# Three edits to the order of loads, weight splits and products between a hybrid layer's out-projection and its first feed-forward matrix

## The chip, the cores and the metric

The kernel runs on 1 core of one Trainium2 chip. Its time is the device time of one execution in microseconds (us). One matmul instruction is issued after the other on TensorE (PE); VectorE (DVE), ScalarE (ACT) and GpSimd (POOL) prepare its operands and take its results; SyncE (SP) issues most loads, and ACT and POOL issue some of the stores.

## The reference

One decoder layer on x of 2048 tokens by 1024 channels, float32:

```python
def rmsnorm(x, g):
    r = lax.rsqrt(jnp.mean(xf * xf, axis=-1, keepdims=True) + EPS)
    return xf * r * g
...
h = rmsnorm(x, g1)
mixed = concat(mLSTM heads (chunkwise, stabilised) * gate, S5 state space * GLU)
x = x + mixed @ w_out                                # out-projection
x = x + square(relu(rmsnorm(x, g2) @ w1)) @ w2       # feed-forward, 4096 wide
return rmsnorm(x, gf)
```

All products are kept at about float32 accuracy: each operand is split into a high part (a rounded copy, made by ACT) and a low part (operand minus high part, made by DVE or POOL), and each product is the sum of three matmuls, high by high, high by low, low by high.

## The kernel before

The program has four stages: the mixer, then the out-projection with the second norm, then the first feed-forward matrix (FFN1), then the second one (FFN2) with the final norm. A tile scheduler sets the order in which each engine runs its instructions, from the order of the code and from its own estimates; so code that is moved changes the order on engines other than those it names. Buffers come from pools of fixed size, and a load into a buffer waits for the last reader of what was in it.

**Out-projection.** Four tiles of 512 tokens (`o_tile(t)`), in each four column blocks `j` of 256, so 16 units of 96 matmuls (L913 to L915) that accumulate into `po` and are added to x (L917). The weights of a unit come from `wunit` (L91): for t = 0 a raw 1 MB load (`wraw`, one buffer in this stage), two copies by ACT into `whi` (L103), and two subtractions into `wlo` (L108), the first half of the columns on POOL and the second on DVE; then `whi` and `wlo` are written to DRAM (W_dx, L111 and L112). For t = 1 to 3, `whi` and `wlo` are loaded from there (L96, L97), 2 MB for a unit. `whi` and `wlo` have two buffers each. The results of a tile go to DRAM by four writes that POOL issues (X_d, L919). Behind tiles 0 and 1 stands `first_norm`, which normalises, transposes and splits the operands of the first half of FFN1 (B11, B21, T1, T2, B22), and writes two more, T3 and T4, to DRAM (HT_d, L961).

**FFN1.** Two halves of the tokens, 16 f-blocks in each (`ff1(half, f)`, L1017), and in each f-block seven products of blocks in place of eight (a Strassen-Winograd scheme), every one 12 matmuls of 512 columns into one PSUM bank (`pf`, L1046 to L1048): 84 matmuls. The products go by the operand of the token side: B11, B21, T1, T2, B22, T3, T4. The weight side of an f-block is one 1 MB load (`raw`, L1020, one buffer); four sums of its quarters on DVE (`sw`, L1033 to L1037); and splits (L866 on ACT, L867 on DVE): `wa` for the products with B11 and B21, `wb` for T1 and T2, `wc` for B22 and T3, and `wd`, from a quarter of `raw` itself, for T4, each with one buffer. The seventh product of an f-block (T4) with the work behind it (`rest`) is put on a list, and `fourth()` runs it in the next f-block, behind the products with B11 and B21; at the end of each half `fourth()` is called once more. Results leave for DRAM by stores that ACT issues, three of 256 KB for `c` and one of 1 MB for `ss` (A_d, L1087). Ahead of the first f-block the code loads T3 and T4 (`sg`, L1095, eight loads of 256 KB) and the norm's weights `gb` (L1097). Between the halves the operands of the second half (`hraw`, L1107, seven loads of 1 MB through two buffers) are loaded and split with one instruction of 2048 columns for each part.

Of the kernel before, what the change touches and what calls it, by code (L numbers as in the profile page):

```python
# [43 lines left out]
def tile_hybrid_block(ctx, tc, x, xT, wqk, wv, wo, wu, wglu, wout, w1, w2,  # L44
# [47 lines left out]
    def wunit(src, n, lo_eng, parts=2, key=None, keep=False):  # L92
        hi = wp.tile([P, 2080], F32R, tag="whi", name="whi")
        lo = wp.tile([P, 2080], F32R, tag="wlo", name="wlo")
        if key in split_d:
            Y.dma_start(out=hi[:, :n].bitcast(F32), in_=split_d[key][0])  # L96
            Y.dma_start(out=lo[:, :n].bitcast(F32), in_=split_d[key][1])  # L97
            return hi, lo
        raw = wraw(src, n)
        h = n // parts  # L100
        for i in range(parts):
            s = slice(i * h, (i + 1) * h)
            S.activation(hi[:, s], raw[:, s], AF.Copy)  # L103
            e = lo_eng[i % len(lo_eng)]
            q = h // 1 if e is G else h
            for j in range(0, h, q):
                s = slice(i * h + j, i * h + j + q)
                e.tensor_tensor(lo[:, s], raw[:, s], hi[:, s].bitcast(F32), op=SUB)  # L108
        if keep:
            split_d[key] = dram.tile([2, P, n], F32, name=f"W_d{key}")  # L110
            Y.dma_start(out=split_d[key][0], in_=hi[:, :n].bitcast(F32))  # L111
            Y.dma_start(out=split_d[key][1], in_=lo[:, :n].bitcast(F32))  # L112
        return hi, lo
# [777 lines left out]
    def o_tile(loaded):  # L891
        t, mxs, mdma = loaded
        xts = []
        for j in range(4):
            wh, wl = wunit(wout[j].rearrange("p k n -> p (k n)"), 2048, (G, V), key=f"x{j}", keep=t == 0)
            if j == 0:
                for c in range(NC):
                    i = (0, 1, 4, 5, 2, 3)[(4 * t + c) % 6]
                    xt = oa[i // 2].tile([P, DM], F32, tag=f"acc{i}", name="acc")
                    with tc.issue_after(mdma.ins):  # L900
                        Y.dma_start(out=xt, in_=x[t * TT + c * P:t * TT + (c + 1) * P, :])
                    xts.append(xt)
            wh = wh[:, :2048].rearrange("p (k n) -> p k n", k=KD)
            wl = wl[:, :2048].rearrange("p (k n) -> p k n", k=KD)
            js = slice(j * 256, (j + 1) * 256)
            pss = [bank_a("po") for _ in range(NC)]
            for ks in ([(0, 4), (4, 8)] if j in (0, 3) else [(0, 8)]):
                for c in range(NC):
                    cs = slice(c * P, (c + 1) * P)
                    for k in range(*ks):  # L910
                        o = pss[c][:, 0:256]
                        ah, al = mxs[k]
                        T.matmul(o, ah[:, cs], wh[:, k, :], start=(k == 0), stop=False)  # L913
                        T.matmul(o, ah[:, cs], wl[:, k, :], start=False, stop=False)  # L914
                        T.matmul(o, al[:, cs], wh[:, k, :], start=False, stop=(k == 7))  # L915
            for c in range(NC):
                V.tensor_tensor(xts[c][:, js], pss[c][:, 0:256], xts[c][:, js], op=ADD)  # L917
        for c in range(NC):
            G.dma_start(out=X1_d[t][c], in_=xts[c])  # L919
        return xts  # L920
# [61 lines left out]
    with ExitStack() as st:  # L982
# [21 lines left out]
            for i, n in enumerate(OPS):  # L1004
                G.dma_start(out=HD_d[i][:, :, cs], in_=sg[n])

        last = []
        nf = [0]

        def bank_f():  # L1010
            nf[0] += 1
            return ps_.tile([P, TT], F32, tag="gsn"[nf[0] % 3], name="pf")

        def fourth():
            if last:
                last.pop()()

        def ff1(half, f):
            raw = rwp.tile([P, 4, TT], F32, tag="raw", name="raw")
            Y.dma_start(out=raw, in_=w1[f])  # L1020
            sw = rwp.tile([P, 4, TT], F32, tag="sw", name="sw")
            a11, a12, a22, a21 = [raw[:, i] for i in range(4)]
            s1, s2, s4, s3 = [sw[:, i] for i in range(4)]
# [31 lines left out]
            def add(o, ps, c):  # L1055
                V.tensor_tensor(o, ps, c, op=ADD)  # L1056

            def keep(i, c):
                S.dma_start(out=A_d[half][f // 4][i][:, f % 4, :], in_=c)
# [4 lines left out]
            add(c11, prod("12", "B21"), u)  # L1064
            sq(c11)
            keep(0, c11)
            fourth()
            p5 = prod("S1", "T1")
            add(u, prod("S2", "T2"), u)
            add(c12, p5, u)  # L1070
# [8 lines left out]
            V.tensor_tensor(ss[:, 1], ss[:, 0], c11, op=SUB)  # L1079
            V.tensor_tensor(ss[:, 2], c11, c12, op=SUB)  # L1080

            def rest():
                add(c21, prod("22", "T4"), u)
                sq(c21)
                keep(1, c21)
                V.tensor_tensor(ss[:, 3], c21, ss[:, 1], op=SUB)
                S.dma_start(out=A_d[half][f // 4][3:7, :, f % 4, :].rearrange("i p n -> p i n"), in_=ss)  # L1087
            last.append(rest)

        gb = stg.tile([P, DM], F32, tag="gb", name="gb")  # L1090
        for i, n in enumerate(("T3", "T4")):
            H[n] = pair(hb, n)
# [3 lines left out]
                split(*[x[:, :, c * P:(c + 1) * P] for x in H[n]], sg)  # L1096
        Y.dma_start(out=gb, in_=g2v[0].partition_broadcast(P))  # L1097
        for f in range(NF):
            ff1(0, f)
            if f % 2 == 1 and f < 8:  # L1100
                chunk2(f // 2)
        stg_cm.__exit__(None, None, None)
        fourth()
        stg = fpool("st1", 2)
        for i, n in enumerate(OPS):
            raw = stg.tile([P, 4, TT], F32, tag="hraw", name="hraw")
# [2 lines left out]
            split(*H[n], raw)  # L1109
        for f in range(NF):  # L1110
            ff1(1, f)
        fourth()
    right_cm.__exit__(None, None, None)
    ps_cm.__exit__(None, None, None)

# [176 lines left out]
```

## Time and profile before

| | |
|---|---|
| median of 3 runs | 2285.95 us (2281.8 to 2290.44) |
| profiled execution | 2285.07 us, span from first to last instruction 2283.3 us |
| mean granted TensorE clock, share of full speed | 0.976 |
| busy, share of the span | PE 94%, DVE 70%, ACT 41%, POOL 14% |
| chain that ended last, by engine | PE 58%, DMA 17%, DVE 16%, issue 4%, ACT 3% |
| stages, us from the start of the span | mixer to 740, out-projection to 961, FFN1 from 978 to 1637, FFN2 from 1645 |

A stage with a busy PE is bound by the number of matmuls; what an edit to the order can change is the time in which PE has nothing to do or runs at its lower clock. So the waits of PE, what ended them, and the granted clock after them are the rows to look at, stage by stage. A share of DMA near 1.0 in a stretch says that its 16 engines were moving data all the time.

### The profile page before, as it was taken

The numbers are of one execution on the slowest core, as the hardware profiler recorded it, in microseconds if no ns is written. First come the engines' busy times: TensorE is split into PE (matmuls) and PEld (weight loads), VectorE is DVE, ScalarE is ACT, GpSimd is POOL, SyncE is SP. The second block draws the span as 40 slices with busy tenths as digits, with TensorE's granted clock in tenths as the row PEclk, the third lists the DMA queues.
The fourth block names the chain that finished last, engine by engine and source line by source line (L and its number), as shares of the span: only waits on it lengthen the run. The fifth ranks groups of instructions, "written<-read, shape, count | busy, mean of one in ns | idle before, by whom it ended". The sixth has DMA issues, their size and how long they took to land.

```text
span 2283.3 us, 29089 instructions
## 1 busy us (share of the span) xinstructions
PE 2157.2 (94%) x11092; PEld 1821.9 (80%) x11092; DVE 1601.0 (70%) x2286; ACT 943.4 (41%) x1368; POOL 309.5 (14%) x307
## 2 busy tenths in 40 slices
PE   8889999999999999889999999999899999999997
PEld 6677888897887899767777777777688888788886
DVE  8966777775666447167776776666666779877688
ACT  5454434333444322055454554444443334533333
POOL 3674333121121101001100000000000000000000
PEclk9989999999999899989999999999999999999999
DMA  6488677776666877646564553444754344744332
GB/s 237 132 224 258 210 243 253 242 213 209 211 219 226 326 301 298 242 154 227 182 214 147 196 195 117 143 146 152 252 229 160 143 148 166 275 149 153 149 122 92
DMA packets 182467, 454.14 MB, mean 199 GB/s; under 512 B 53140, under 2 KB 82340, under 8 KB 151480
## 3 DMA queue, kind: packets, MB, share of 16 engines
q1 hardware_dynamic: 141784, 367.28, 48.2%
q10 hardware_dynamic: 35360, 67.18, 7.7%
q0 software_dynamic: 5184, 17.83, 2.0%
q8 instruction: 87, 1.43, 0.3%
q14 instruction: 52, 0.43, 0.1%
HBM read 311.56 MB, written 140.66 MB: 198 GB/s over the span
## 4 chain that ended last, share of the span: by engine, by line
PE 58%; DMA 17%; DVE 16%; issue 4%; ACT 3%; POOL 1%; SPq 1%; ACTq 0%; DVEq 0%; POOLq 0%
PE pp L1168 9%; PE pp L1167 9%; PE pp L1166 9%; DMA raw<-in_w 8%; PE pf L1046 4%; PE pf L1048 4%; PE pf L1047 4%; PE po L915 2%; PE po L913 2%; PE po L914 2%; DMA whi<-W_dx 2%; PE pg L792 2%; PE pg L793 1%; DVE w1l L867 1%; PE pg L794 1%
## 5 line engine op out<-in xcount | busy, mean ns | idle before, releaser
L1056 DVE TENSOR_TENSOR c<-pf,c 128x512 f32<-128x512 f32 x224 | 153.4, 686 | 79.4 <-PE pf L1048 74.8
L1172 DVE TENSOR_TENSOR m<-pp,m 128x1024 f32<-128x1024 f32 x96 | 116.8, 1219 | 97.0 <-PE pp L1168 96.9
L1166 PE MATMUL pp<-b0h,a0h 128*128 128x512 f32 x448 | 173.8, 392 | 7.4 <-ACT a0h L866 7.4
L1167 PE MATMUL pp<-b1l,a1h 128*128 128x512 f32 x448 | 177.1, 395 | 2.4 <-DVE b1l L867 2.4
L1168 PE MATMUL pp<-b0h,a0l 128*128 128x512 f32 x448 | 175.1, 392 | 1.8 <-DVE a0l L867 1.8
L1168 PE MATMUL pp<-b1h,a1l 128*128 128x512 f32 x448 | 176.8, 395 | 0.0
L1167 PE MATMUL pp<-b0l,a0h 128*128 128x512 f32 x448 | 175.5, 392 | 0.0
L1166 PE MATMUL pp<-b1h,a1h 128*128 128x512 f32 x448 | 174.8, 395 | 0.0
L118 PE MATMUL pg<-whi,hTh 128*128 128x260 f32 (+1 forms) x512 | 152.3, 297 | 6.9 <-DVE Gt L191 6.1
L1202 POOL TENSOR_TENSOR rr<-rr,cst 128x2 f32<-128x2 f32 x8 | 6.0, 756 | 1107.0 <-DVE rr L1201 1097.1
L913 PE MATMUL po<-whi,mxh 128*128 128x256 f32 x512 | 147.6, 290 | 7.4 <-DMA whi<-W_dx 4.9
L119 PE MATMUL pg<-wlo,hTh 128*128 128x260 f32 (+1 forms) x512 | 150.5, 294 | 0.0
L915 PE MATMUL po<-whi,mxl 128*128 128x256 f32 x512 | 146.7, 289 | 4.0 <-DVE mxl L887 4.0
L120 PE MATMUL pg<-whi,hTl 128*128 128x260 f32 (+1 forms) x512 | 150.0, 293 | 0.0
L914 PE MATMUL po<-wlo,mxh 128*128 128x256 f32 x512 | 146.9, 288 | 0.0
L866 ACT ACTIVATE a1h<-af 128x2048 fp32r<-128x2048 f32 x28 | 53.7, 1919 | 180.8 <-PE pp L1167 152.5
L866 ACT ACTIVATE w1h<-raw 128x1024 fp32r<-128x1024 f32 x64 | 53.9, 844 | 171.2 <-DMA raw<-in_w 128.1
L866 ACT ACTIVATE a0h<-af 128x2048 fp32r<-128x2048 f32 x28 | 53.7, 1918 | 163.1 <-PE pp L1167 148.3
L1052 ACT ACTIVATE c<-c 128x512 f32<-128x512 f32 x128 | 80.2, 628 | 93.6 <-DVE c L1056 91.8
L118 PEld LDWEIGHTS pg<-whi,hTh 128*128 128x128 f32 x512 | 100.3, 196 | 9.3 <-DVE Gt L191 6.8
L913 PEld LDWEIGHTS po<-whi,mxh 128*128 128x128 f32 x512 | 99.9, 195 | 8.9 <-DMA whi<-W_dx 3.4
L1166 PEld LDWEIGHTS pp<-b0h,a0h 128*128 128x128 f32 x448 | 84.8, 189 | 25.5 <-ACT a0h L866 7.8
(370 smaller groups left out, 6146.5 us busy)
## 6 DMA issues: line engine op xcount, KB each, us to landing
af<-A_d SPq DMA_DIRECT2D x56, 1024.0 KB, 4.8
raw<-in_w SPq DMA_DIRECT2D x32, 1024.0 KB, 6.6
A_d<-ss ACTq DMA_DIRECT2D x32, 1024.0 KB, 8.5
A_d<-c ACTq DMA_DIRECT2D x96, 256.0 KB, 3.4
fB<-in_w SPq DMA_DIRECT2D x24, 1024.0 KB, 5.5
xraw<-in_xT SPq DMA_DIRECT2D x27, 512.0 KB, 5.0
whi<-W_dq SPq DMA_DIRECT2D x12, 1024.0 KB, 5.8
wlo<-W_dq SPq DMA_DIRECT2D x12, 1024.0 KB, 5.5
```

Of the source, the lines that this page charges most:

```text
L118: T.matmul(ps, ah, bh, start=(i == 0), stop=False)
L119: T.matmul(ps, ah, bl, start=False, stop=False)
L120: T.matmul(ps, al, bh, start=False, stop=(i == n - 1))
L866: S.activation(hi, src, AF.Copy)
L913: T.matmul(o, ah[:, cs], wh[:, k, :], start=(k == 0), stop=False)
L914: T.matmul(o, ah[:, cs], wl[:, k, :], start=False, stop=False)
L915: T.matmul(o, al[:, cs], wh[:, k, :], start=False, stop=(k == 7))
L1056: V.tensor_tensor(o, ps, c, op=ADD)
L1166: T.matmul(o, ah[:, k, cs], bh[:, k, :], start=(k == 0), stop=False)
L1167: T.matmul(o, ah[:, k, cs], bl[:, k, :], start=False, stop=False)
L1168: T.matmul(o, al[:, k, cs], bh[:, k, :], start=False, stop=(k == 3))
L1172: e.tensor_tensor(o, s, o, op=ADD)
```

## The change

Three parts. In `o_tile`, `wunit` loses its key: the weights of each of the 16 units are loaded raw and split anew, nothing is written to W_dx and nothing is loaded from it. In `ff1`, the seventh product and the work behind it stand at the end of their own f-block, and `fourth()` and its list are gone. And the raw weights of the first f-block are loaded (`raw0`) in the code ahead of the loads of T3, T4 and `gb`.

```diff
@@ o_tile
-            wh, wl = wunit(wout[j].rearrange("p k n -> p (k n)"), 2048, (G, V), key=f"x{j}", keep=t == 0)
+            wh, wl = wunit(wout[j].rearrange("p k n -> p (k n)"), 2048, (G, V))
@@ ff1
-        def fourth():
-            if last:
-                last.pop()()
-
-        def ff1(half, f):
+        def w1_load(f):
             raw = rwp.tile([P, 4, TT], F32, tag="raw", name="raw")
             Y.dma_start(out=raw, in_=w1[f])
+            return raw
+
+        def ff1(half, f, raw=None):
+            raw = w1_load(f) if raw is None else raw
...
             sq(c11)
             keep(0, c11)
-            fourth()
             p5 = prod("S1", "T1")
...
-            def rest():
-                add(c21, prod("22", "T4"), u)
-                sq(c21)
-                keep(1, c21)
-                V.tensor_tensor(ss[:, 3], c21, ss[:, 1], op=SUB)
-                S.dma_start(out=A_d[half][f // 4][3:7, :, f % 4, :].rearrange("i p n -> p i n"), in_=ss)
-            last.append(rest)
-
+            add(c21, prod("22", "T4"), u)
+            sq(c21)
+            keep(1, c21)
+            V.tensor_tensor(ss[:, 3], c21, ss[:, 1], op=SUB)
+            S.dma_start(out=A_d[half][f // 4][3:7, :, f % 4, :].rearrange("i p n -> p i n"), in_=ss)
+
+        raw0 = w1_load(0)
         gb = stg.tile([P, DM], F32, tag="gb", name="gb")
...
-            ff1(0, f)
+            ff1(0, f, raw0 if f == 0 else None)
...
-        fourth()
         stg = fpool("st1", 2)
```

What it makes of the order is seen at three places. The first is the queue of SP at the passage from the out-projection (L86 to L97, and `wraw`, are its weights) to FFN1 (`raw` is the weight load of an f-block, `sg` the loads of T3 and T4 from HT_d, `xt` a load for the norm of the second half). Before:

```order
L97 DMA wlo<-W_dx_8069 128x2048
L96 DMA whi<-W_dx_8069 128x2048
L1095 DMA sg<-HT_d_91 128x512 x4
L1097 DMA gb<-in_g2v 128x1024
L1020 DMA raw<-in_w 128x2048
L993 DMA xt<-X_d_82 128x1024
L1095 DMA sg<-HT_d_92 128x512 x4
L1020 DMA raw<-in_w 128x2048 x2
```

Now:

```order
L86 DMA wraw<-in_wout 128x2048
L1015 DMA raw<-in_w 128x2048
L1092 DMA sg<-HT_d_91 128x512 x4
L1094 DMA gb<-in_g2v 128x1024
L993 DMA xt<-X_d_82 128x1024
L1015 DMA raw<-in_w 128x2048
L1092 DMA sg<-HT_d_92 128x512 x4
L1015 DMA raw<-in_w 128x2048
```

The first weight load of FFN1 went from behind five loads to the place right behind the last weight load of the out-projection, and the second came ahead of T4's loads.

The second place is PE's queue at the passage from one f-block to the next in the second half (names as above; `h` and `l` are the high and low parts). Before, the last matmuls of one block's sixth product and the first of the next block:

```order
L1048 MATMUL pf<-T3h,w1l 128x512
L1046 MATMUL pf<-B11h,w1h 128x512
L1047 MATMUL pf<-B11l,w1h 128x512
L1046 MATMUL pf<-B21h,w1h 128x512
L1047 MATMUL pf<-B21l,w1h 128x512
L1046 MATMUL pf<-T1h,w1h 128x512
L1047 MATMUL pf<-T1l,w1h 128x512
L1046 MATMUL pf<-T2h,w1h 128x512
```

Now, the last of one block's seventh product and the first of the next block:

```order
L1046 MATMUL pf<-T4l,w1h 128x512
L1047 MATMUL pf<-T4h,w1l 128x512
L1045 MATMUL pf<-B11h,w1h 128x512
L1046 MATMUL pf<-B11l,w1h 128x512
L1047 MATMUL pf<-B11h,w1l 128x512
```

Before, two matmuls of each of four products stood ahead of the first that reads a low part of the weights, and T4 of the block stood behind products of the next; now the products stand whole, one behind the other, with T4 last.

The third place is PE's queue at the change of the halves. Before, the last f-block's seventh product and then the first matmuls with the second half's B11 and B21:

```order
L1047 MATMUL pf<-T4l,w1h 128x512
L1048 MATMUL pf<-T4h,w1l 128x512
L1046 MATMUL pf<-B11h,w1h 128x512
L1047 MATMUL pf<-B11l,w1h 128x512
L1046 MATMUL pf<-B21h,w1h 128x512
L1047 MATMUL pf<-B21l,w1h 128x512
L1048 MATMUL pf<-B11h,w1l 128x512
```

Now (B11, T1, T2 and B21 here are the second half's; T4 is still the first half's):

```order
L1046 MATMUL pf<-B11l,w1h 128x512
L1047 MATMUL pf<-B11h,w1l 128x512
L1045 MATMUL pf<-T4h,w1h 128x512
L1045 MATMUL pf<-T1h,w1h 128x512
L1046 MATMUL pf<-T1l,w1h 128x512
L1045 MATMUL pf<-T2h,w1h 128x512
L1046 MATMUL pf<-T2l,w1h 128x512
L1045 MATMUL pf<-B21h,w1h 128x512
```

The second half's first product stands ahead of the seventh of the first half now, and behind that one's first matmul come two each with T1 and T2 of the second half; its other eleven matmuls stand behind the whole product with B21.

## Rows read from the trace of the kernel before

**Rows 1.** The windows of the span by stage: out-projection, first half of FFN1, second half. Columns: from and to, length, busy us (and instructions) of PE, PE's weight loads, DVE, ACT and POOL, granted PE clock, DMA share, GB/s.

```profile
740.00:975.00 235.00, 205.68 (x1644) 203.10 (x1644) 103.29 (x188) 54.16 (x94) 28.55 (x37) 0.93 0.76 293
975.00:1297.00 322.00, 313.39 (x1356) 250.34 (x1357) 234.20 (x335) 160.38 (x248) 26.89 (x36) 0.99 0.52 176
1297.00:1635.00 338.00, 328.06 (x1387) 260.82 (x1386) 235.83 (x318) 161.56 (x221) 0.00 (x0) 0.99 0.50 168
```

**Rows 2.** The waits of PE: the first row from the window 740 to 980, the second from 975 to 1300, the third from 1300 to 1640. Columns: what waited and for what, us in total, times, longest.

```profile
PE po L913 <- DMA whi<-W_dx: 4.9, 3, 2.1
...
PE pf L1046 <- ACT w1h L866: 22.4, 12, 16.7
...
PE pf L1046 <- ACT w1h L866: 7.6, 12, 2.3
```

**Rows 3.** The chain that ended last, between 1500 and 1560, in the second half of FFN1. Columns: start, us, what.

```profile
1518.43 0.47 PE pf L1048 x2
...
1525.55 6.69 DMA raw<-in_w
...
1535.36 0.50 PE pf L1046
...
1545.78 6.84 DMA raw<-in_w
```

**Rows 4.** The timeline of one f-block of the first half: PE, ACT and SP. Columns: start, us, engine, line, operation, out and in, in brackets the idle time before it and what ended it.

```profile
1146.32 0.50 PE L1046 MATMUL pf<-T1h,w1h 128*128 128x512 f32 x1 [0.79 <-ACT w1h L866]
...
1154.09 0.39 PE L1048 MATMUL pf<-T4h,w1l 128*128 128x512 f32 x1
...
1155.59 0.61 ACT L866 ACTIVATE w1h<-raw 128x512 fp32r<-128x512 f32 x1
...
1156.96 0.33 SPq L1020 DMA_DIRECT2D raw<-in_w  x1
```

**Rows 5.** The chain that ended last, from the out-projection's last matmul to the first of FFN1 and on.

```profile
961.00 0.13 PE po L915
...
961.87 3.97 DMA X_d<-acc
...
968.31 8.30 DMA raw<-in_w
976.69 1.06 ACT w1h L866
977.80 0.80 PE pf L1046
...
983.60 0.43 PE pf L1047
...
984.54 0.23 PE pf L1046
```

**Rows 6.** The timeline of PE, the first matmul with T1 in the first f-block.

```profile
986.48 0.40 PE L1046 MATMUL pf<-T1h,w1h 128*128 128x512 f32 x1
```

**Rows 7.** The timeline at the change of the halves: PE at the start of the last f-block of the first half, DVE and ACT at the splits of the second half's operands, PE at the end of T4, and at the first and the last slow matmul behind it.

```profile
1286.47 0.40 PE L1046 MATMUL pf<-B11h,w1h 128*128 128x512 f32 x1
...
1294.42 2.28 DVE L867 TENSOR_TENSOR B11l<-hraw,B11h 128x2048 fp32r<-128x2048 f32 x1
...
1302.64 1.92 ACT L866 ACTIVATE T1h<-hraw 128x2048 fp32r<-128x2048 f32 x1 [1.82 <-DMA hraw<-HD_d]
...
1307.23 1.92 ACT L866 ACTIVATE T2h<-hraw 128x2048 fp32r<-128x2048 f32 x1 [2.67 <-DMA hraw<-HD_d]
...
1308.97 0.39 PE L1048 MATMUL pf<-T4h,w1l 128*128 128x512 f32 x1
...
1311.70 0.80 PE L1046 MATMUL pf<-B11h,w1h 128*128 128x512 f32 x1 [2.35 <-ACT w1h L866]
...
1318.47 0.43 PE L1048 MATMUL pf<-B11h,w1l 128*128 128x512 f32 x1
```

**Rows 8.** The timeline from FFN1 to FFN2: PE's last matmul of FFN1, a DVE instruction of the last f-block, PE's first matmul of FFN2.

```profile
1637.34 0.39 PE L1048 MATMUL pf<-T4h,w1l 128*128 128x512 f32 x1
...
1638.41 0.69 DVE L1080 TENSOR_TENSOR ss<-c 128x512 f32<-128x512 f32 x1 [5.42 <-DMA A_d<-ss]
...
1645.10 0.79 PE L1166 MATMUL pp<-b0h,a0h 128*128 128x512 f32 x1 [7.37 <-ACT a0h L866]
```

**Rows 9.** The DMA issues between 735 and 1000, those of the out-projection's weights. Columns: out and in, queue, operation and count, KB each, median us from issue to landing.

```profile
whi<-W_dx SPq DMA_DIRECT2D x12, 1024.0 KB, 11.7
...
wraw<-in_wout SPq DMA_DIRECT2D x4, 1024.0 KB, 8.1
```

**Rows 10.** The timeline of ACT, POOL, DVE and PE in the first two units of the out-projection: the splits of their weights, and the first matmul.

```profile
743.19 2.00 ACT L103 ACTIVATE whi<-wraw 128x1024 fp32r<-128x1024 f32 x2 [1.06 <-DMA wraw<-in_wout]
744.33 2.36 POOL L108 TENSOR_TENSOR wlo<-wraw,whi 128x1024 fp32r<-128x1024 f32 x1 [4.92 <-ACT whi L103]
745.23 2.54 DVE L108 TENSOR_TENSOR wlo<-wraw,whi 128x1024 fp32r<-128x1024 f32 x1 [2.38 <-ACT whi L103]
746.77 0.58 PE L913 MATMUL po<-whi,mxh 128*128 128x256 f32 x1
...
761.90 1.21 DVE L108 TENSOR_TENSOR wlo<-wraw,whi 128x1024 fp32r<-128x1024 f32 x1
```

**Rows 11.** One of the windows of 10 us in the out-projection, behind its second tile. Columns as in Rows 1.

```profile
890.00:900.00 10.00, 10.00 (x87) 10.00 (x85) 9.27 (x19) 2.38 (x4) 1.13 (x2) 1.00 0.50 203
```

More of the change, by code (lines that the diff above doesn't have):

```diff
@@ L1005, in chunk2 @@
                 G.dma_start(out=HD_d[i][:, :, cs], in_=sg[n])
-        last = []
         nf = [0]
@@ L1111, in tile_hybrid_block @@
             ff1(1, f)
-        fourth()
     right_cm.__exit__(None, None, None)
```

## The prediction

> **What bounds the kernel now.** I read the windows by stage first, then the waits of PE in each stage, then the chain of waits, then the timeline where PE stands still. The change touches the out-projection, FFN1 and its two ends; the mixer keeps its order, and FFN2 but for its start. In the windows [rows 1] PE is idle for 29.3 us of the out-projection's 235, for 8.6 of the first half's 322 and for 9.9 of the second half's 338: so 48 us is all that the edits could win there. The waits [rows 2] say on whom. In FFN1 it is nearly always the split `w1h` of a weight block: 22.4 us in the first half, of which one wait of 16.7 is the start, and 7.6 in the second, of which 2.3 is the change of halves. That leaves 5.7 and 5.3 us in 11 waits each, one of about 0.5 us in most f-blocks.
>
> The chain [rows 3] shows what makes these short waits: a raw load runs on it in every f-block, 6.7 us, and from one such load to the next it is 1545.78 - 1525.55 = 20.23 us. PE's own work in an f-block is 84 matmuls of 0.233 us (a pair takes 0.47 [rows 3]), 19.6 us. So the block is paced by a ring, 0.63 us longer than PE: the one raw buffer is held until the split for T4 has read it, that split waits for its own buffers, which the T4 product of the block before frees, and this product stands a quarter into the block. The timeline shows the ring's links [rows 4]: T4's last matmul at 1154.09, the split of the last quarter at 1155.59, the next load at 1156.96.
>
> **Part 1, the seventh product in its own f-block.** T4 of a block now ends where the next begins. The split for T4 and the next load can then go about 3 us into a block (1156.96 - 1154.09 = 2.9, [rows 4]); the load takes 6.7 us and PE starts 3.1 us behind its landing (1525.55 + 6.69 to 1535.36, [rows 3]), 13 us together, of 19.6. The ring opens and PE sets the pace. Per wait that wins the 0.63 us: 22 x 0.63 = **14 us**. The bounds are the bare waits, 11.0, and 0.63 for each of 30 blocks, 19. What is added is a chance for a wait at T4, whose sum, square and 1 MB store now follow at the end of the block. On ACT's queue the store waits for DVE, and behind it stand the next block's splits; their buffers hold a whole block's lead by then, so I cost that at nothing. If that cover is gone, the 0.5 us wait comes back, which is one of the rivals.
>
> At the end of FFN1 the same move takes out a wait: DVE stood 5.42 us for the store of the block before to leave `ss`, and PE started FFN2 at 1645.10, 7.5 us behind its last matmul at 1637.34 [rows 8]. The store will be issued some 8 us earlier and that wait goes; the sum behind T4 and FFN2's first splits are next. I take **-2.5 us**, bounds 0 and -5.
>
> **Change of halves.** Here the order speaks against the change. Before, PE ran T4 of the last block until 1308.97, waited 2.35 us and ran at the lower clock until 1318.47 [rows 7]: 13 matmul steps or so at half speed, about 3 us, and 6.4 with both waits. Now the queue has two matmuls each with the second half's T1 and T2 ahead of B21 and of the rest of T4. From the block's start (1286.47) PE comes there after 85 matmuls, six products, the second half's first and T4's first, at +19.8 us. But T2's high part ended at 1309.15, which is +22.7, and its low part, 2.28 us by its like, at +25.0 [rows 7]; with the splits in DVE's new order, each 2.28 us behind the ones of B11 and B21 and two buffers for seven loads, I get +28.2. So PE will stand 4.7 to 7.9 us with eleven ready matmuls of T4 and a whole product behind it in its queue, then run some steps at the lower clock (3 us, as now), and the splits of the operands behind T2 come later by as much (some 3 us, my choice). From 14 in place of 6.4 I take **+8 us**, bounds +1 and +12.
>
> **Part 2, raw0 ahead.** The start of FFN1 is the chain at its plainest [rows 5]: the last matmul at 961.00, the last tile's last store, 3.97 us, whose buffer the loads of T3 take over, five DMA issues, raw at 968.31, landing 8.30 us later, a split, and PE starts at 977.80 and runs at the lower clock (0.43 us a matmul) until about 984. The first matmul with T1 runs at 986.48 [rows 6]. In the new queue of SP raw0 stands ahead of all that. It waits only for a store of the tile before, so it lands while the out-projection's last unit still runs. The sums in `sw` share a buffer with a store that ends at about 964.4 (one 1.44 us ahead of the 961.87 one, with its 3.97 us); behind it lie three sums and the low split, some 3 us, so PE has all it needs at 967.5. Its 20 matmuls left then take 7.4 us, most at the lower clock as now, and T1 begins at 975. That wins **11 us** (986.48 - 975, less half a us). It could be 7, if T4's operand, whose loads now stand behind another 1 MB, comes late for the end of the first block (needed at 986; I get 983 to 985), or 12.
>
> **Part 3, the weights split again.** Removed are eight stores and 24 loads of 1 MB, the latter 11.7 us in the median for a `whi` [rows 9], and with them the 4.9 us in which PE waited for W_dx [rows 2]. Added are 12 loads of 1 MB, 24 copies of 1.0 us on ACT, 12 subtractions of 2.4 us on POOL and 12 on DVE of 1.21 us [rows 10]. One raw buffer makes a new ring: issue, load (8.1 us [rows 9]) and split, 743.19 to the end of POOL's part at 746.69 and DVE's at 747.77, 4.6 us [rows 10]: 13.1 us. PE takes (961.00 - 746.77) / 16 = 13.4 us a unit [rows 5, 10]. So the ring hides, barely, behind PE, and I take **-5 us**. Below, all the idle time of this stage but the 16.7 goes: 29.3 - 16.7 = 12.6. Above, see the rivals.
>
> The first DVE subtraction took 2.54 us, while POOL worked on its own half; in the second unit DVE took 1.21 [rows 10]. The Trainium skill says why this may not be chance: "SBUF — State Buffer", section "Who interferes with whom", has DVE instructions with two SBUF inputs and GpSimd instructions that read SBUF share one port and block each other for a whole instruction. The trace agrees in these rows. By it the new POOL work, 12 x 2.4 us, would each time hold up DVE, which has the second norm beside it; that is the second rival.
>
> **The sum.** -14 - 2.5 + 8 - 11 - 5 = -24.5 us on the profiled 2285.07, which lies 0.9 below the median: 2285.07 - 24.5 = 2260.6, and by the median 2261.4. I say **2261**.
>
> **The rivals.** *The new order costs nothing* (0.15): the operands of the second half come in time for T1 and T2, so +8 is 0, and the out-projection loses twice the 4.9 since half the DMA traffic for its weights is gone: -14 - 2.5 - 11 - 10 = -37.5, 2248 us. For it: DMA share 0.76 in that stage [rows 1]. Against: the splits' durations in [rows 7] are DVE's own, not waits.
>
> *DVE is the bound of the out-projection* (0.12): beside the second norm DVE is busy 9.27 of 10 us [rows 11]. If three to five of the twelve subtractions fall there and take 2.5 us, PE waits for accumulations or transposes 7.5 to 12.5 us in place of winning 5: -12 to -7, 2274 to 2279 us. Against: DVE is busy for 103 of the stage's 235 us [rows 1].
>
> *The ring does not open* (0.10): DVE or ACT come to the next splits late, behind T4's sum and the store, and the short waits stay: -10.5, 2275 us. That is also what is left if the change does not do what it says. Against: the freed load has 6 us to spare.
>
> *Slower, by the single raw buffer in the out-projection* (0.07): a unit costs L + 5.0 us where L is the load's landing time, so all 16 grow by L - 8.4. The other terms give back 19.5, so it decides from L = 8.4 + 19.5 / 16 = 9.6 us on. At the 11.7 us of the W_dx loads it costs 16 x 3.3 = 53, in all +33: 2319 us. For it: 11.7 is what loads of this size took in this very stage. Against: they came in pairs, with 2 MB a unit where there is 1 now, and raw loads took 8.1.
>
> **How the numbers follow.** The forecast has 0.54; 0.02 lie elsewhere. Low and high: the term bounds move the sum by some 10 us either way without the rivals, the first rival reaches 2248 and below, the second and third 2279. From 2244 to 2280 leaves out the fourth and the tails, less than 2 in 10. A measurement of this kernel can tell about 0.5% from no change, 11.4 us, so faster is under 2274.5. The forecast and the first rival lie there, with nearly half of the second and a part of the third: 0.77. The rest of these two is the same, 0.16; the fourth is slower, 0.07.
>
> **What would show it.** Right: no wait for `w1h` of 0.5 us in the steady blocks, raw issued 3 us into a block, and a period of 19.6; T1's first matmul of FFN1 14 us behind the last of the out-projection, not 25; a wait of PE of 5 to 8 us for T1 or T2 at the change of halves; `wraw` landing in about 8 us. Wrong: waits for `wlo` or `whi` by PE in the out-projection, of a us or more a unit; a subtraction on DVE of 2.5 us in most units with PE waiting behind it; or PE idle at T4 in every block. The forecast fails as a whole if the out-projection takes longer than 221 us from its first matmul to its last, for 214 before.

## The result, and the profile after

| | before | after |
|---|---|---|
| median | 2288.19 us (2281.8 to 2291.13, 4 runs) | 2228.88 us (2227.55 to 2232.78, 4 runs) |
| ratio | | 0.9747, 95% interval 0.9721 to 0.9773 |
| profiled execution, span | 2283.3 us | 2227.6 us |
| granted TensorE clock, mean | 0.976 | 0.980 |

The kernel got 59 us faster. The forecast was 25 us, and its range ended at 2244. So the direction held and the size did not; the question of the experiments is where the other 34 us came from.

Landmarks cut the two spans into pieces. They are the starts of matmuls in the timeline of PE: the first and last with `po`, the first with T1, in each f-block the first with B22 as its mark (blocks are counted from 0, the second half is 16 to 31), the last with T4, the first and last with `pp`. The pieces that are left out (from T1 to block 1, from block 31 to the last T4, and behind the last `pp`) changed by 0.5 us at most. The first and the last matmul of each piece stand at the same place in PE's order before and after.

| piece, us | before | after | difference | forecast |
|---|---|---|---|---|
| mixer, to the first `po` | 746.8 | 741.9 | -4.9 | 0 |
| out-projection, first to last `po` | 214.1 | 196.1 | -17.9 | -5 |
| from there to T1 of the first f-block | 25.6 | 14.5 | -11.2 | -11 |
| blocks 1 to 14, in the first half | 269.4 | 260.0 | -9.4 | |
| blocks 19 to 31, in the second half | 242.0 | 233.6 | -8.4 | -14 with the row above |
| blocks 14 to 19, over the change of halves | 106.4 | 100.9 | -5.5 | +8 |
| last T4 to the first `pp` | 7.8 | 6.6 | -1.2 | -2.5 |
| first to last `pp` | 625.8 | 628.0 | +2.2 | 0 |

**The out-projection.** The windows from its first to its last matmul, before and then after (columns as in [rows 1]), hold the same 1628 matmuls:

```profile
747.00:961.00 214.00, 201.57 (x1628) 199.62 (x1628) 97.25 (x179) 46.61 (x82) 25.66 (x35) 0.96 0.75 292
```

```profile
742.00:938.00 196.00, 194.93 (x1628) 194.14 (x1628) 126.50 (x191) 71.07 (x108) 58.43 (x47) 1.00 0.60 217
```

Before, PE was idle for 12.4 us, and its busy time was 6.6 us longer for the same work, since the granted clock was 0.96 and not 1.00. After, idle time is 1.1 us. DVE does 29 us more and POOL 33, and the DMA share falls from 0.75 to 0.60. The waits of PE before that [rows 2] leaves out, in the window 740 to 980, are those for the splits of the mixer's results (`mr`, split into `mxh` and `mxl`):

```profile
PE po L915 <- DVE mxl L887: 4.0, 2, 3.3
PE po L913 <- ACT mxh L886: 2.3, 2, 1.5
```

With the 4.9 us for `whi<-W_dx` they are 11.2 of the 12.4 us. Behind the waits that end at 764.37, 811.80 and 873.82 PE ran 17 to 20 matmuls each at the lower clock; behind the one that ends at 926.47 it did not. All these waits lie in windows of 10 us with a DMA share of 1.02 to 1.04; two of these windows (columns as in [rows 1]):

```profile
757.00:767.00 10.00, 5.93 (x38) 5.51 (x37) 7.60 (x17) 4.36 (x7) 3.33 (x2) 0.76 1.04 409
922.00:932.00 10.00, 8.00 (x67) 7.83 (x67) 0.85 (x3) 0.00 (x0) 0.00 (x0) 1.00 1.03 427
```

After, in the window 740 to 940:

```profile
PE po L913 <- DVE acc L917: 0.6, 1, 0.6
PE po L915 <- DVE mxl L887: 0.5, 1, 0.5
```

The DMA issues between 735 and 940 of the kernel after, and one of before, between 735 and 1000 (columns as in [rows 9]): the weights come in 4.8 us, and `mr`, which everything in a tile waits for, in 8.2 in place of 10.4. These are medians of the few loads whose landing the trace has, three of `wraw` and six of `mr`, and those of `mr` spread from 4 to 11 us after and from 4 to 15 before.

```profile
wraw<-in_wout SPq DMA_DIRECT2D x15, 1024.0 KB, 4.8
mr<-MX_d SPq DMA_DIRECT2D x16, 512.0 KB, 8.2
```

```profile
mr<-MX_d SPq DMA_DIRECT2D x16, 512.0 KB, 10.4
```

**Start of FFN1.** The timeline of PE and DVE, to be read beside [rows 5, 6]:

```profile
938.02 0.28 PE L915 MATMUL po<-whi,mxl 128*128 128x256 f32 x1
...
941.84 0.69 DVE L1032 TENSOR_TENSOR sw<-raw 128x512 f32<-128x512 f32 x1 [3.07 <-DMA X_d<-acc]
...
943.65 1.82 DVE L867 TENSOR_TENSOR w1l<-raw,w1h 128x1024 fp32r<-128x1024 f32 x2
...
944.92 0.79 PE L1047 MATMUL pf<-B11h,w1l 128*128 128x512 f32 x1 [5.69 <-DVE w1l L867]
...
952.48 0.40 PE L1045 MATMUL pf<-T1h,w1h 128*128 128x512 f32 x1
```

No load is waited for any more. What is left is the wait that the forecast named: the sums `sw` lie where a store of the last tile has to end first, and the low part of the weights stands behind them on DVE.

**Steady blocks.** The chain that ended last, from 1500 to 1545, by line: it is PE alone, where a raw load ran on it in every block before [rows 3].

```profile
by line: PE pf L1045 33.5%; PE pf L1046 33.5%; PE pf L1047 33.4%
```

A block takes 19.47 us in the second half, PE's own time, in place of about 20.2.

**Change of halves.** The timeline of PE and DVE, beside [rows 7]:

```profile
1265.05 0.39 PE L1047 MATMUL pf<-T4h,w1l 128*128 128x512 f32 x1
1265.28 0.40 PE L1045 MATMUL pf<-B11h,w1h 128*128 128x512 f32 x1
...
1266.30 2.29 DVE L867 TENSOR_TENSOR T1l<-hraw,T1h 128x2048 fp32r<-128x2048 f32 x1 [1.90 <-ACT T1h L866]
...
1268.65 0.50 PE L1046 MATMUL pf<-T1l,w1h 128*128 128x512 f32 x1 [0.17 <-DVE T1l L867]
...
1270.85 2.28 DVE L867 TENSOR_TENSOR T2l<-hraw,T2h 128x2048 fp32r<-128x2048 f32 x1
...
1274.36 0.40 PE L1046 MATMUL pf<-T2l,w1h 128*128 128x512 f32 x1
...
1288.36 0.40 PE L1045 MATMUL pf<-T4h,w1h 128*128 128x512 f32 x1
1288.59 0.40 PE L1045 MATMUL pf<-T1h,w1h 128*128 128x512 f32 x1
1288.82 0.40 PE L1046 MATMUL pf<-T1l,w1h 128*128 128x512 f32 x1
```

T4 of the last block of the first half ends at 1265.28, and the second half begins at once with whole products. The low part of T1 is ready at 1268.59, and PE waits 0.17 us for it; that of T2 is ready at 1273.13, and PE comes to it at 1274.36. In the window 1260 to 1300 the granted clock is 1.00 (it was 0.91 between 1300 and 1340 before), and all of PE's waits are these, 2.5 us:

```profile
PE pf L1045 <- ACT w1h L866: 1.2, 1, 1.2
PE pf L1047 <- DVE w1l L867: 0.6, 1, 0.6
PE pf L1046 <- DVE B22l L867: 0.5, 1, 0.5
PE pf L1046 <- DVE T1l L867: 0.2, 1, 0.2
```

**FFN1 to FFN2.** The timeline of PE and DVE, beside [rows 8]: 1.2 us less. DVE still waits for the store of `ss`, 4.25 us in place of 5.42.

```profile
1579.98 0.69 DVE L1078 TENSOR_TENSOR ss<-c 128x512 f32<-128x512 f32 x1 [4.25 <-DMA A_d<-ss]
1580.08 0.39 PE L1047 MATMUL pf<-T4h,w1l 128*128 128x512 f32 x1
1586.66 0.80 PE L1161 MATMUL pp<-b0h,a0h 128*128 128x512 f32 x1 [6.20 <-ACT a0h L866]
```

The chain shows the store itself, before and then after:

```profile
1628.08 10.24 DMA A_d<-ss
```

```profile
1565.29 14.60 DMA A_d<-ss
```

It was issued 14.8 us ahead of PE's last matmul of FFN1, where it had been 9.3, but took 4.4 us longer, with a DMA share of 1.00 from 1565 to 1575. So by the same measure it ended only 1.2 us earlier, which is what the piece won.

### The profile page after: what moved, and what is told of

Same layout as the page of the kernel before. It is cut to its first block, busy times and chain, and to the rows that moved or that the text cites. A ratio compares the mean times of both kernels' runs of the same rounds, so it can differ in the third digit from the quotient of the medians.

```text
span 2227.6 us, 29189 instructions
## 1 busy us (share of the span) xinstructions
PE 2140.1 (96%) x11092; PEld 1814.6 (81%) x11092; DVE 1632.8 (73%) x2298; ACT 959.2 (43%) x1392; POOL 344.2 (15%) x319
## 4 chain that ended last, share of the span: by engine, by line
PE 73%; DVE 11%; DMA 8%; issue 4%; ACT 2%; POOL 1%; SPq 1%; POOLq 0%; DVEq 0%; ACTq 0%
PE pp L1163 9%; PE pp L1162 9%; PE pp L1161 9%; PE pf L1047 9%; PE pf L1046 8%; PE pf L1045 8%; PE pg L792 2%; PE pg L794 2%; PE pg L793 2%; PE pg L118 1%; PE pg L119 1%; PE pg L120 1%; PE po L913 1%; PE po L914 1%; PE po L915 1%
## 5 line engine op out<-in xcount | busy, mean ns | idle before, releaser
L108 POOL TENSOR_TENSOR wlo<-wraw,whi 128x1024 fp32r<-128x1024 f32 (+1 forms) x42 | 108.2, 2585 | 121.3 <-ACT whi L103 119.2
```

## The experiments

Theory F is the forecast with its own terms; theory R reads the pieces above as the parts' own effects, with the out-projection's gain coming from the traffic that part 3 took out.

### Each part alone

e1 is the kernel before with the first hunk of the diff alone:

```diff
-            wh, wl = wunit(wout[j].rearrange("p k n -> p (k n)"), 2048, (G, V), key=f"x{j}", keep=t == 0)
+            wh, wl = wunit(wout[j].rearrange("p k n -> p (k n)"), 2048, (G, V))
```

> The kernel before with part 3 alone (out-projection weights loaded raw and split for each tile). Theory F, the forecast's term: 5 us are won, the waits for W_dx (ratio 0.998). Theory R, read from the landmarks of the two traces: the out-projection from its first to its last matmul goes from 214 to 196 us, since all its waits and the lower clock behind them go with the W_dx traffic, so 18 us are won (ratio 0.992) and this stage has a granted clock of 1.00. The mixer, whose order is the same, is not shorter by the 5 us that its end came earlier in the trace of the changed kernel.

e2 is the kernel before with the seventh product in its own f-block alone:

```diff
-            fourth()
             p5 = prod("S1", "T1")
...
-            def rest():
-                add(c21, prod("22", "T4"), u)
+            add(c21, prod("22", "T4"), u)
```

> The kernel before with part 1 alone (seventh product in its own f-block). Theory F: -14 for the steady blocks, -2.5 at FFN2, +8 at the change of halves, in all -8.5 us (ratio 0.996) with a wait of PE of 5 to 8 us for T1 or T2 between the halves. Theory R: the steady blocks win 17 us, the change of halves wins 5 in place of losing 8, since the second half begins with whole products behind the first half's T4; with 1 to 2 us at the end of FFN1, in all -23 us (ratio 0.990).

e3 is the kernel before with raw0 alone:

```diff
+        raw0 = w1_load(0)
         gb = stg.tile([P, DM], F32, tag="gb", name="gb")
...
-            ff1(0, f)
+            ff1(0, f, raw0 if f == 0 else None)
```

> The kernel before with part 2 alone (raw0 loaded ahead of T3, T4 and gb). Both theories: the first matmul with T1 comes 14 to 15 us behind the out-projection's last, not 25.6, so -11 us (ratio 0.995). A rival: with T4 of the first block put behind the next block's first products as before, the gain is given back in the first two blocks, within 3 us of no change.

e4 is the changed kernel with e1's edit undone:

```diff
-            wh, wl = wunit(wout[j].rearrange("p k n -> p (k n)"), 2048, (G, V))
+            wh, wl = wunit(wout[j].rearrange("p k n -> p (k n)"), 2048, (G, V), key=f"x{j}", keep=t == 0)
```

> The changed kernel with part 3 undone (out-projection weights kept in W_dx and loaded again). Theory F: -19.5 us against the kernel before (ratio 0.9915). Theory R: -34 us (ratio 0.985), with the out-projection at 214 us as before and FFN1 as in the changed kernel: the parts add.

| run | median | ratio to before (95%) | out-projection | to T1 | blocks 1-14 | 14-19 | 19-31 |
|---|---|---|---|---|---|---|---|
| before | 2287.0 | 1 | 214.1 | 25.6 | 269.4 | 106.4 | 242.0 |
| e1, part 3 | 2269.91 | 0.9919 (0.9906 to 0.9932) | 196.0 | 25.2 | 272.2 | 108.9 | 242.7 |
| e2, part 1 | 2261.89 | 0.9886 (0.9868 to 0.9904) | 214.3 | 25.6 | 260.0 | 102.0 | 233.6 |
| e3, part 2 | 2277.97 | 0.9958 (0.9942 to 0.9974) | 215.4 | 14.7 | 272.8 | 107.3 | 242.0 |
| e4, parts 1 and 2 | 2248.23 | 0.9826 (0.9812 to 0.984) | 214.4 | 14.5 | 260.0 | 101.5 | 233.6 |

Each part moves its own pieces, and the others stay but for up to 3.4 us in the blocks of e1 and e3. The three single effects (-0.0081, -0.0114, -0.0042) add to -0.0237, inside the interval of the whole. Theory F falls in e1 (18.5 us won where it had 5), in e2 (26 where it had 8.5; no wait of 5 to 8 us between the halves), and so in e4. Its term for raw0 holds: 9.6 us, and the rival that the next blocks give it back falls. The mixer's end is not part of any: its first `po` lies between 740 and 753 us in these and all later executions with the same mixer code, and the 4.9 us are within that spread. The profiled executions of e1 and e2, with 750.7 and 752.8, lie 6.5 and 8.7 us above their kernels' medians, and that of e3, with 740.1, lies 4.7 below.

### What the traffic of W_dx cost

e5 keeps part 3 and puts 20 MB back into SP's queue, as copies that nobody reads; e10 does so with stores that ACT issues.

```diff
+            for i in range(2 if t == 0 else 1):
+                idle.append(dram.tile([P, 2080], F32, name=f"N_d{len(idle)}"))
+                with tc.issue_after(wdma[-1].ins):
+                    Y.dma_start(out=idle[-1][:, :2048], in_=w2[i, j % 2, t % 2].rearrange("p k n -> p (k n)"))
```

> The changed kernel with 20 copies of 1 MB from DRAM to DRAM in SP's queue, two behind each weight load of the first tile and one behind each of the other tiles; nobody reads them. That is the traffic that part 3 took out (36 transfers of 1 MB became 16), without any operand that waits for it. Theory T, the DMA engines were too full for the loads that PE does wait for: the out-projection goes from 196 us back by 8 to 18 us, with waits of PE for whi, mxh or mxl, so 0.978 to 0.982 of the kernel before. Theory D, only the dependence counted (PE waiting for whi and wlo themselves out of DRAM): within 3 us of the changed kernel, 0.975.

```diff
+            for i in range(2 if t == 0 else 1):
+                idle.append(dram.tile([P, 2080], F32, name=f"N_d{len(idle)}"))
+                S.dma_start(out=idle[-1][:, :2048], in_=wh[:, :2048].bitcast(F32))
```

> The changed kernel with 20 stores of 1 MB of whi to DRAM that nobody reads, issued by ACT and not by SP. If the 16 DMA engines' time is what the W_dx traffic took (theory T), the out-projection goes back to about 210 us as with the copies in SP's queue, 0.981 to 0.985. If it was the place in SP's queue, ahead of the loads that PE waits for, it stays within 4 us of 196, 0.975 to 0.977.

e5: 2254.38 us, 0.9846 (0.9829 to 0.9863), out-projection 212.1 us. e10: 2257.12 us, 0.9856 (0.9834 to 0.9879), out-projection 222.5 us. In e5 24 of the mixer's matmuls that run inside this stage in the other kernels come ahead of its first `po`, so its 212.1 us hold less work. From one matmul of the mixer's end that stands at the same place in all four orders (the 3901st of PE, at 711.7 us after) to the last `po` it is 244.1 us before, 226.3 after, 249.3 in e5 and 253.2 in e10. The windows of that stretch, in this order:

```profile
716.00:961.00 245.00, 228.10 (x1756) 221.64 (x1754) 118.73 (x220) 60.91 (x106) 31.20 (x41) 0.96 0.73 281
```

```profile
711.00:938.00 227.00, 221.38 (x1755) 216.06 (x1755) 147.78 (x232) 85.20 (x131) 63.69 (x53) 0.98 0.60 216
```

```profile
714.00:963.00 249.00, 228.77 (x1750) 221.98 (x1749) 147.03 (x231) 82.81 (x125) 61.08 (x50) 0.95 0.73 277
```

```profile
714.00:967.00 253.00, 230.75 (x1751) 223.43 (x1750) 145.51 (x231) 82.05 (x126) 59.75 (x51) 0.95 0.72 273
```

PE's idle time in them is 16.9, 5.6, 20.2 and 22.3 us. Both runs are back at about the DMA share and the lower clock of the kernel before, and above its idle time. No operand waits for these bytes, so theory D falls; and it is much the same from another engine's queue, so it is not a place in SP's queue. So bytes that nobody reads are enough to bring back what part 3 won.

By what way they reach PE is not the same in the three. Of the 13.7 us that PE waited in e5 from 750 on, most are waits for DVE's accumulations, and not for the names that were expected:

```profile
PE po L919 <- DVE acc L923: 8.1, 5, 3.4
PE po L919 <- ACT mxh L888: 2.8, 1, 2.8
PE po L921 <- DVE mxl L889: 1.2, 1, 1.2
```

The longest, 3.36 us, ends at 836.59: four accumulations stand in DVE's order behind a subtraction of the weights that took 2.80 us and two splits of the norm. In e10 `wraw` landed in 8.0 us in the median in place of 4.8, and PE waited 5.2 us for accumulations, 3.7 for `whi` and 2.8 for `wlo`; ACT's copy ahead of the longest of these had itself waited 12.6 us for the raw load.

```profile
wraw<-in_wout SPq DMA_DIRECT2D x15, 1024.0 KB, 8.0
```

`mr` shows no common way: 12.3 us in e10 and 6.9 in e5, each from three loads whose landing is known. Both runs cost more in time than expected, and by the four stretches above both cost more than W_dx did, 23 and 27 us for 18; why was not followed up.

How full the engines were before, one more window of 10 us inside the out-projection shows:

```profile
870.00:880.00 10.00, 7.92 (x55) 7.68 (x54) 7.45 (x14) 3.57 (x8) 1.13 (x2) 0.83 1.03 418
```

The Trainium skill, "DMA: Bandwidth & Descriptors", section "Where 436 GB/s comes from", puts the ceiling of the 16 ports through which DMA traffic reaches SBUF, the core's own memory, at some 435 GB/s; the 418 of this row, at a share of 1.03, agrees. The same section of the Trainium skill has transfers between HBM (the DRAM) and SBUF bound lower, at some 358 GB/s; this row, whose transfers (`whi`, `wlo`, `acc`, HT_d) are of that kind, went above it.

### Which ring set the block

e6 leaves T4 in the next f-block, as before, and gives the splits that it reads two buffers, which frees the raw buffer earlier:

```diff
-                hi, lo = [p.tile([P, len(names), TT], F32R, tag=tag, name="w1" + x) for p, x in ((whp, "h"), (wlp, "l"))]
+                hi, lo = [p.tile([P, len(names), TT], F32R, tag=tag, name="w1" + x, bufs=1 + (tag == "wd")) for p, x in ((whp, "h"), (wlp, "l"))]
...
-            u, c11, c12, c22 = [ctp.tile([P, TT], F32, tag=f"c{i}", name="c", bufs=2) for i in range(4)]
+            u, c11, c12, c22 = [ctp.tile([P, TT], F32, tag=f"c{i}", name="c", bufs=2 if i < 2 else 1) for i in range(4)]
```

> The kernel before, T4 still carried into the next f-block, with two buffers for the splits that T4 reads (wd) and, to make room, one buffer in place of two for c12 and c22. If the ring through the raw buffer and these splits set the block's time (theory R), the period falls to PE's 19.5 us and some 19 us are won, 0.9915, without moving the product; the change of halves stays as in the kernel before, or wins a little. If the place of the product itself counts (rival: DVE and ACT come late to the splits as long as T4's sum stands among them), the period stays near 20.2 and the time within 4 us of the kernel before.

2281.62 us, 0.9964 (0.9948 to 0.998): 8 us won, between the two. The waits for `w1h` are gone from the steady blocks and the change of halves takes 99.5 us, so the ring through `raw` was there as the forecast said. But blocks 19 to 31 take 237.4 us, not 233.6, and the chain between 1500 and 1545 shows a second ring behind the first:

```profile
1508.24 8.47 DMA A_d<-ss
...
1527.86 8.77 DMA A_d<-ss
```

With T4 carried, the 1 MB store of `ss` leaves late, and the next block's `ss` waits for it: one such store every 19.62 us. Blocks 1 to 14 took 277.3 us, 7.9 more than before, since two of them took 27 to 29 us each; that may be the single buffers of c12 and c22, and was not followed up, so the time of e6 is not the price of one ring alone. Moving T4 opened both rings at once; two more buffers opened one.

### POOL and DVE in the out-projection, and a mend

e7 and e8 are the changed kernel with one edit each, e11 with both, and e12 is the changed kernel again beside it.

```diff
-            wh, wl = wunit(wout[j].rearrange("p k n -> p (k n)"), 2048, (G, V))
+            wh, wl = wunit(wout[j].rearrange("p k n -> p (k n)"), 2048, (V,))
```

> The changed kernel with both halves of the out-projection's low parts on DVE, none on POOL. DVE's subtraction of 128x1024 takes 1.2 us each time, not 2.35 in the mean, so 32 of them take as long as 16 did; PE does not wait in this stage either way, so the time is the changed kernel's within 3 us (0.975). If POOL's hold on DVE did cost PE time there (the rival of the forecast), 4 us or more are won.

```diff
-        ctp, hb, whp, wlp, rwp = [fpool(n) for n in ("ct", "hb", "wh", "wl", "rw")]
+        ctp, hb, whp, wlp, rwp, wdp = [fpool(n) for n in ("ct", "hb", "wh", "wl", "rw", "wd")]
...
-                hi, lo = [p.tile([P, len(names), TT], F32R, tag=tag, name="w1" + x) for p, x in ((whp, "h"), (wlp, "l"))]
+                hi, lo = [(wdp if tag == "wd" else p).tile([P, len(names), TT], F32R, tag=tag + x, name="w1" + x) for p, x in ((whp, "h"), (wlp, "l"))]
```

> The changed kernel with the splits for T4 (wd) in a pool of their own behind the raw buffer, so that the weight sums sw of the first f-block lie where no store of the last tile's results has to end first. PE's wait of 5.7 us at the start of FFN1 and part of the lower clock behind it go: 4 to 8 us less than the changed kernel, 0.972. If the low part of the weights is late for another reason, nothing changes, 0.975.

> The changed kernel with both mends, the low parts of the out-projection's weights on DVE alone and the wd splits in a pool of their own. By the landmarks of the two runs apart: 1.6 us less in the out-projection, 6 less in FFN1, up to 2 more at FFN2's start: 5 to 6 us faster than the changed kernel beside it, 0.972. If the gain in FFN1 is given back, no difference.

> The changed kernel itself, as the neighbour of the three others: 0.9747 as before, within 0.0015.

e7: 2228.73 us, 0.9733 (0.9715 to 0.975). The subtractions on DVE, by form, in the window 735 to 940 (line, engine, operation, names, shapes and count, busy us, mean ns), after and then e7:

```profile
L108 DVE TENSOR_TENSOR wlo<-wraw,whi 128x1024 fp32r<-128x1024 f32 x16 | 37.5, 2346 | 20.3 <-ACT whi L103 19.8 <-issue 0.5
```

```profile
L108 DVE TENSOR_TENSOR wlo<-wraw,whi 128x1024 fp32r<-128x1024 f32 x32 | 38.4, 1220 | 9.1 <-ACT whi L103 9.1
```

Beside POOL, 16 subtractions took DVE as long as 32 without it. The Trainium skill's rule, in "SBUF — State Buffer", section "Who interferes with whom", that a DVE instruction with two SBUF inputs and a GpSimd instruction that reads SBUF block each other, is borne out by these rows. It cost the kernel nothing that its time shows, since e7's is the changed kernel's; the out-projection took 194.6 us, where the two profiles of the changed kernel have 196.1 and 197.9.

e8: 2229.97 us, 0.974 (0.9719 to 0.9761); e11: 2227.37 us, 0.9725 (0.9703 to 0.9747); e12: 2231.18 us, 0.974 (0.9717 to 0.9763; one execution of 4270 us is left out of the interval), as expected. In the traces e8 and e11 do what was meant: the wait of 5.69 us is gone, and the 25th matmul behind the last of the out-projection starts 5.8 us behind it in both, not 14.5. (T1 can't be the mark here, since its first matmul is the 5th there and the 25th in the changed kernel.) Part of it goes back at the next block, where PE waits 1.78 us for the low part of its weights. FFN1 from the last of the out-projection to its last T4 takes 636.2 and 635.5 us where the changed kernel takes 642.1 and 641.6 (e12). In the time this is not shown: the intervals overlap, and in e11's profiled execution the mixer alone ended 7.8 us later than in e12's.

### The same edit in the mixer

e9 is the changed kernel with the mixer's query and key weights loaded raw and split anew as well:

```diff
-            wh, wl = w3(wunit(wqk[h].rearrange("p k n -> p (k n)"), 2048, (G,), key=f"q{h}", keep=t == 0))
+            wh, wl = w3(wunit(wqk[h].rearrange("p k n -> p (k n)"), 2048, (G,)))
```

> The changed kernel, with part 3's edit made to the mixer's query and key weights as well: the 12 reloads of 2 MB from W_dq and its 8 stores are replaced by 12 raw loads of 1 MB, split on ACT and POOL. Theory T (traffic costs where PE waits for loads): the mixer's PE waits for DMA by 1.4 us only, so nothing is to be won there, and POOL, busy for 250 of the mixer's 740 us and blocking DVE, gets 12 x 4.8 us more: 0 to 12 us slower than the changed kernel, 0.975 to 0.980. The rival rule, a raw load and a new split always beat a stored split: 5 us or more faster, below 0.9725.

2252.2 us, 0.984 (0.981 to 0.9871): some 21 us slower than the changed kernel beside it, more than expected; the first `po` lies at 764.1 us, and the later stages take what they took. The windows of the mixer, after and e9, and its largest group on DVE in both:

```profile
0.00:740.00 740.00, 684.94 (x4018) 598.71 (x4019) 531.03 (x1123) 322.82 (x617) 249.71 (x227) 0.97 0.70 223
```

```profile
0.00:740.00 740.00, 673.73 (x3932) 587.98 (x3933) 543.34 (x1085) 335.05 (x627) 296.63 (x247) 0.96 0.63 191
```

```profile
L659 DVE SCALAR_TENSOR_TENSOR acc<-xin,hv,acc 128x512 f32<-128x512 f32 x96 | 78.9, 824 | 8.1 <-ACT acc L657 6.7 <-POOL xin L653 0.6
```

```profile
L659 DVE SCALAR_TENSOR_TENSOR acc<-xin,hv,acc 128x512 f32<-128x512 f32 x90 | 91.1, 1015 | 5.2 <-ACT acc L657 4.7
```

The DMA share falls here too, from 0.70 to 0.63, but PE had waited only 1.4 us for DMA there. POOL's new subtractions hold up DVE, whose instruction at L659 goes from 824 to 1015 ns in the mean: up to 770 us, 15 of the 96 overlap a subtraction of POOL in e9, and 5 in the changed kernel; these take 2.18 and 2.01 us in the mean, the others 0.78 and 0.76. And in the mixer PE's longest waits are for DVE (8.0 and 7.0 us after, 8.5 and 7.8 in e9). ACT's new copies add to it, with 12 us more busy time; what each costs was not separated.

## Why the prediction was right in direction and wrong in size

**Out-projection: a term mis-sized, -18 where it had -5, and beyond its bound of -12.6.** The step that failed is "with them the 4.9 us in which PE waited for W_dx". It credited part 3 with the waits that name W_dx alone. They were 4.9 of the 12.4 us of idle time; 6.3 more carry the names mxh and mxl, and the busy time at the lower clock was another 6.6. After, 1.1 us of idle time and a clock of 1.00 are left. e5 and e10 show that the traffic by itself brings this price back; through which load it reached PE before is argued from the full windows, not shown. The bound failed as well, because "all the idle time" leaves out time in which PE is busy at half speed; the clock of 0.93 stood in [rows 1] and was not turned into microseconds. The new ring was never near: the load landed in 4.8 us, not 8.1, in a stage with a DMA share of 0.60 in place of 0.75.

**Change of halves: a misreading, -5.5 where it had +8.** The step that failed is "Now the queue has two matmuls each with the second half's T1 and T2 ahead of B21 and of the rest of T4". The rows shown as the third place of the order after, ahead of the prediction, are those from the first block of the second half to its second, one f-block too late; their T4 is the second half's. In the trace they are the ones at 1288.36 and on, and nothing waits there. At the real change whole products of B11, T1 and B21 stand ahead of the low part of T2. The ready times of the operands were about right (T2's low part at +28.2 us from the start of the last block by the forecast, 1273.13 - 1245.81 = +27.3 in the trace, that block having begun at 1245.81); the place of the matmuls that need them was not. The piece holds five blocks, and by the mean of blocks 19 to 31 (20.17 us before, 19.47 after) 3.5 of the 5.5 us are the ring's, as in any five blocks. What the change costs on top went from 5.6 us to 3.6, where the forecast had it going from 6.4 to 14: the lower clock is gone, which lasted until 1318.47 behind PE's wait for `w1h` [rows 7], and waits of 2.5 us are left. In e6, with the ring opened and T4 still carried, one wait of 1.56 us for `w1h` is left and the granted clock stays at 1.00.

**Steady blocks: right mechanism, 18 where it had 14.** The term was mis-sized: it counted 0.63 us for the 22 blocks in which PE's wait was listed, and 0.7 us in the mean were won in each of the 25 blocks of the two rows. The bound of 19 held. e6 shows a second ring, through `ss`, which the forecast did not have and which the same move opens.

**Start of FFN1: right**, 11.2 and in e3 11.0 us. **FFN2: half the size, and a step that failed**, 1.2 for 2.5. "The store will be issued some 8 us earlier and that wait goes" did not happen: it was issued 5.5 us earlier, took 4.4 longer, and 4.25 of the 5.42 us of waiting stayed.

**The rivals.** That POOL holds up DVE is real (2.35 us for 1.22) and hidden in the changed kernel; in e5, with raw loads that land in 7.2 us in the median in place of 4.8, PE's waits for accumulations, which this rival named, come to 8.1 us. The raw ring in the out-projection did not come near its point of 9.6 us. The first rival, that nothing new is paid, was the nearest, and still 19 us too high, since it too had the out-projection too small.

Of the single execution's differences the mixer's -4.9 and FFN2's +2.2 (628.0 us, where e12, the same kernel, has 625.4) belong to no part; why the mixer's end moves by up to 13 us between executions stays open.

## What to carry to other kernels

A split operand kept in DRAM and loaded again saves two engines some work and costs twice the bytes. Here splitting it anew paid in a stage whose DMA share was 0.75, with PE's waits in stretches at 1.0, and did not in the mixer (0.70), where PE waited for the engines that would do the splitting. So ask first which of the two PE waits for. Count a stage's price in idle time and in busy time at the lower clock together, and count every wait that falls into a stretch with full DMA engines, not only those that carry the name of the load that goes. When a store is issued earlier, ask whether it also ends earlier. When an order is read without times, find the block by counting from the start of the stage before resting a term on it.

## What had not been expected of the hardware

20 MB that nobody reads, put into a stage of 196 us, cost 23 us as copies issued by SP (e5) and 27 as stores issued by ACT (e10), from the same matmul ahead of the stage to its end. A 1 MB store that was issued 5.5 us earlier ended only 1.2 us earlier, both against the last matmul of FFN1 (it took 14.60 us in place of 10.24). The same 1628 matmuls took PE 201.6 us busy at a granted clock of 0.96 and 194.9 at 1.00. Profiled executions with the same mixer code differ by up to 13 us in the mixer alone.
